# Latent attention of a two-layer trunk: second rotary product behind the first queries, latent keys' transposes one a quantum, rotary work in single steps

## The chip, the cores and the metric

One core of a Trainium2 chip runs the whole program in one launch. The metric is the device time of one execution in microseconds; the median of several runs counts. In profiles the engines are PE (TensorE matmuls; PEld its weight loads), DVE (VectorE), ACT (ScalarE), POOL (GpSimd) and SP (SyncE, which issues the DMAs).

## The reference, cut to what matters

Two decoder layers at 256 tokens, width 2048, float32. Layer 0 has block-sparse attention and a gated MLP, layer 1 has multi-head latent attention and the same kind of MLP. The change lies in the latent attention alone:

```python
cq = rms_norm(h @ wq_a, g_qa)                                # 2048 -> 512
q = (cq @ wq_b).reshape(B, S, H, NOPE + RD)                  # 16 heads of 128 + 64
q_nope = rms_norm(q[..., :NOPE], g_qn)
q_rope = rope(rms_norm(q[..., NOPE:], g_qr), pos, RD)        # RD = 64
kv_a = h @ wkv_a                                             # 2048 -> 512 + 64
ckv = rms_norm(kv_a[..., :MLA_KV_RANK], g_kva)
k_rope = rope(rms_norm(kv_a[..., MLA_KV_RANK:], g_kr)[:, :, None, :], pos, RD)[:, :, 0]
kv = (ckv @ wkv_b).reshape(B, S, H, NOPE + VD)
k_nope = rms_norm(kv[..., :NOPE], g_kn)
v = kv[..., NOPE:]
# per head: s = (q_nope k_nope + q_rope k_rope) * scale, causal; softmax; s @ v; then @ wo
```

## The kernel before, in words

**Products.** Every weight matrix is streamed from HBM in units of 1 MB (four pieces of 128 x 512; wkv_a in pieces of 128 x 288). The list `units` gives the order. For each piece ScalarE rounds a high part (`whi`, L104) and VectorE subtracts it to get a low part (`wlo`, L105); TensorE multiplies high by high, low by high and high by low. A product with one piece of weights is a quantum: six matmuls in the form of `tok_major` (L235; tokens on the partitions, weights moving), or twelve in that of `feat_major` (L261 to L263).

**Order.** The list `quanta` holds the products in order; `at(q, f)` hangs a piece of other work behind quantum q. At the end one loop writes the program out: for each quantum it first splits the weight piece that is three quanta ahead, then issues the quantum's matmuls, then all work hung at q, in the order in which it was hung. Each engine works through its instructions in this order, so a VectorE instruction that waits holds up the low parts behind it. Parts have five buffers.

**Latent attention.** Its stages in order: wq_a (feature-major, 16 quanta, gives `cqT`); the first rotary product `rotary_queries(0)` (4 quanta: 8 heads of 64); wkv_a (two halves of 16 quanta, 288 columns each, gives `ckv`); then four groups of four heads, each with queries (`mla_wqn`, from `cqT`), keys (`mla_wkn`) and values (`mla_wv`, both from `ckvT`), four quanta each. The first group takes queries first, the others keys first. The second rotary product stands ahead of the second group.

**Work around the change.** Of each product of heads, `Heads.evac` copies the sums out of PSUM on ScalarE, `squares` sums squares per head on VectorE (L379), `rstd` forms the inverse root (GpSimd's power, L392), `scaled` multiplies it in (L397, VectorE; `scaled_only`, L413, on ScalarE for the rotary queries), `rotate` applies the rotary tables on VectorE (L435 to L440), `turned` transposes on TensorE (L449) and `turned_out` copies out on ScalarE (L457, L460). For the latent keys `kva_evac`, `kva_stats`, `kva_scale` (L858, L859), `kva_rotate` (L872 to L876), `kva_turn` (transposes L881, then high and low parts L886 and L887 into `ckvT`) and `kr_turn` (transposes L894, zeroing L898, copies L899 into two tiles, `kr`) do the same. `Head.plan` hangs scores, softmax and values of a head over eight quanta.

With Q for the last quantum of wkv_a, the statistics are hung at Q, the scaling at Q+3, the turns 0 and 1 at Q+3, 2 and 3 at Q+4, the key's rotation at Q+7 and its turn, with the zeroing, at Q+9.

Of the kernel before, what the change touches and what calls it, by code (L numbers as in the profile page):

```python
# [17 lines left out]
P = 128  # L18
# [97 lines left out]
def trunk(ctx: ExitStack, tc: tile.TileContext, a, out):  # L116
# [99 lines left out]
    def at(q, f, *args):  # L216
        side.setdefault(q, []).append((f, args))
# [135 lines left out]
    class Heads:  # L353
# [19 lines left out]
                else:  # L373
                    nc.scalar.activation(dst, src, AF.Copy, scale=self.scale()[:, t : t + 1])

        def squares(self, t):
            for i in range(self.n):
                junk = att_pool.tile([P, P], F32, name="junk", bufs=2)
                nc.vector.tensor_tensor_reduce(  # L379
                    out=junk[:, : self.dh], in0=self.x[:, t, i], in1=self.x[:, t, i], scale=1.0,  # L380
                    scalar=0.0, op0=ALU.mult, op1=ALU.add, accum_out=self.ss[:, t, i : i + 1],
                )
# [9 lines left out]
            nc.gpsimd.tensor_tensor(self.r, ms, mhalf[:, : NT * n], op=ALU.pow)  # L392

        def scaled(self, t):
            if self.gain_column is not None:
                r = self.r[:, t * self.n : (t + 1) * self.n]
                nc.vector.tensor_tensor(  # L397
                    self.x[:, t], self.x[:, t], r[:, :, None].to_broadcast([P, self.n, self.dh]),
                    op=ALU.mult,
                )  # L400
                return
            g = gains[:, self.gain : self.gain + self.dh]
            for i in range(self.n):
                c = t * self.n + i
                nc.vector.scalar_tensor_tensor(
                    self.x[:, t, i], self.x[:, t, i], self.r[:, c : c + 1], g,
                    op0=ALU.mult, op1=ALU.mult,
                )

        def scaled_only(self, t, heads):  # L410
            for i in heads:
                c = t * self.n + i
                nc.scalar.activation(  # L413
                    self.x[:, t, i], self.x[:, t, i], AF.Copy, scale=self.r[:, c : c + 1]
                )

        def rotate(self, t, stages=(0, 1)):
            if not self.rot:
                return
            n, rot = self.n, self.rot  # L420
            hf = rot // 2
            tb, C, Sn = self.tabs
            ct = tb[:, C + t * rot : C + (t + 1) * rot]
            st = tb[:, Sn + t * rot : Sn + (t + 1) * rot]
            x = self.x[:, t]
            def over(s):
                return s[:, None, :].to_broadcast([P, n, s.shape[1]])

            def part(name):
                r = att_pool.tile([P, 16 * 32], F32, name=name, bufs=2)  # L430
                return r[:, : n * rot].rearrange("p (n r) -> p n r", n=n)

            if 0 in stages:
                t1, t2 = self.rot_parts = part("ro1"), part("ro2")
                nc.vector.tensor_tensor(t1, x[:, :, :rot], over(ct), op=ALU.mult)  # L435
                nc.vector.tensor_tensor(t2[:, :, :hf], x[:, :, hf:rot], over(st[:, :hf]), op=ALU.mult)
            if 1 in stages:
                t1, t2 = self.rot_parts
                nc.vector.tensor_tensor(t2[:, :, hf:], x[:, :, :hf], over(st[:, hf:]), op=ALU.mult)
                nc.vector.tensor_tensor(x[:, :, :rot], t1, t2, op=ALU.add)  # L440

        def turned(self, dst, pair, i0):
# [179 lines left out]
    def plan_heads(q, hs, key, step, out=None, late=0):  # L622

        at(q, hs.evac)
        for t in range(NT):
            at(q + step * (1 + t), hs.squares, t)
        at(q + step * 3, hs.rstd)
# [208 lines left out]
                AF.Copy, scale=n3.rstd[:, t : t + 1],  # L836
            )

    def kva_stats():
        ss = small.tile([P, NT, 2], F32, name="kvss")  # L840
        for t in range(NT):
            for k, (lo, hi) in enumerate(((0, 512), (512, 576))):
                junk = att_pool.tile([P, 512], F32, name="kvjunk", tag="ro1", bufs=2)
                nc.vector.tensor_tensor_reduce(
                    out=junk[:, : hi - lo], in0=env["ckv"][:, t, lo:hi], in1=env["ckv"][:, t, lo:hi],
                    scale=1.0 / (hi - lo), scalar=0.0, op0=ALU.mult, op1=ALU.add,
                    accum_out=ss[:, t, k : k + 1],
                )
        ms = small.tile([P, NT * 2], F32, name="kvms")
        nc.vector.tensor_scalar(ms, ss.rearrange("p t k -> p (t k)"), EPS, None, op0=ALU.add)  # L850
        env["kvr"] = small.tile([P, NT * 2], F32, name="kvr")
        nc.gpsimd.tensor_tensor(env["kvr"], ms, mhalf[:, : NT * 2], op=ALU.pow)

    def kva_scale():
        r = env["kvr"]
        for t in range(NT):
            c = env["ckv"][:, t]
            nc.vector.tensor_scalar(c[:, :512], c[:, :512], r[:, 2 * t : 2 * t + 1], None, op0=ALU.mult)  # L858
            nc.vector.scalar_tensor_tensor(  # L859
                c[:, 512:], c[:, 512:], r[:, 2 * t + 1 : 2 * t + 2], gains[:, G_KR : G_KR + 64],  # L860
                op0=ALU.mult, op1=ALU.mult,
            )

    def kva_rotate():
        env["krr"] = att_pool.tile([P, NT, 2, 64], F32, name="krr", bufs=1)
        for t in range(NT):
            x = env["ckv"][:, t, 512:]
            ct = tab[:, T_LC + t * 64 : T_LC + (t + 1) * 64]
            st = tab[:, T_LS + t * 64 : T_LS + (t + 1) * 64]
            t1 = att_pool.tile([P, 64], F32, name="kro1", bufs=2)  # L870
            t2 = att_pool.tile([P, 64], F32, name="kro2", bufs=2)
            nc.vector.tensor_tensor(t1, x, ct, op=ALU.mult)  # L872
            nc.vector.tensor_tensor(t2[:, :32], x[:, 32:], st[:, :32], op=ALU.mult)
            nc.vector.tensor_tensor(t2[:, 32:], x[:, :32], st[:, 32:], op=ALU.mult)
            for i in range(2):
                nc.vector.tensor_tensor(env["krr"][:, t, i], t1, t2, op=ALU.add)  # L876

    def kva_turn(r):
        tp = ps_tp.tile([P, 512], F32, name="tp")
# [11 lines left out]
    def kr_turn():  # L891
        tp = ps_tp.tile([P, 512], F32, name="tp")
        for t in range(NT):
            nc.tensor.transpose(  # L894
                tp[:, t * P : (t + 1) * P], env["krr"][:, t].rearrange("p i d -> p (i d)"), ident
            )
        for i in range(2):
            nc.gpsimd.memset(env["kr"][i], 0.0)  # L898
            nc.vector.tensor_copy(env["kr"][i][i * 64 : (i + 1) * 64, :], tp[i * 64 : (i + 1) * 64, :S])  # L899


# [58 lines left out]
    def rotary_queries(u, step):  # L960
        state = {}
        for kt in range(4):
            q = add(tok_major, state, lambda: env["cqT"], kt, 3)
        hs = Heads(state, 8, 64, None, 64, None, lambda: cq["scale"])

        def rotate(t, stage):
            hs.tabs = (env["gtab"].rearrange("p a r -> p (a r)"), 0, NT * 64)
# [1 line left out]

        at(q, hs.evac)  # L970
        for t in range(NT):
            at(q + step * (1 + t), hs.squares, t)
        at(q + step * 3, hs.rstd)
        for t in range(NT):
            for half in range(2):
                at(q + step * (6 + 2 * t + half), hs.scaled_only, t, range(4 * half, 4 * half + 4))
            at(q + step * (8 + 2 * t), rotate, t, 0)
            at(q + step * (9 + 2 * t), rotate, t, 1)
        for i0 in (0, 2):
            pair = {}  # L980
            at(q + step * 14 + i0 // 2, lambda p=pair, i0=i0: hs.turned(None, p, i0))
            at(q + step * 14 + i0 // 2, lambda p=pair, i0=i0: hs.turned_out(
                env["qrT"][:, 4 * u : 4 * u + 4], p, i0))
# [184 lines left out]
```

## Time and profile before

| | us |
|---|---|
| median of 3 runs (lowest to highest) | 2096.03 (2095.92 to 2097.42) |
| the profiled execution: time | 2096.73 |
| its span, first to last instruction | 2094.9 |
| PE busy | 2086.9 (100%) |
| PEld busy | 2014.8 (96%) |
| DVE busy | 1403.5 (67%) |
| ACT busy | 1137.7 (54%) |
| POOL busy | 45.6 (2%) |

A matmul's record lasts from its start to the modelled end of its pipeline, and the next one starts before that end, so records overlap; how fast TensorE goes on is read from start to start. In a timeline, a row ends with the idle time ahead of it and what ended that, in brackets, where there was any. In a group of instructions the columns are count, busy time, mean ns of one, idle time of the engine ahead of them and its releaser.

### The profile page before, as it was taken

How to read it: one execution, taken by the hardware profiler on the slowest of the kernel's cores; microseconds unless marked ns; L12 is line 12 of the kernel's file. 1: busy time of each engine (PE TensorE's matmuls, PEld its weight loads, DVE VectorE, ACT ScalarE, POOL GpSimd, SP SyncE). 2: the span in 40 equal slices, each digit the busy share in tenths (PEclk: the TensorE clock that was granted, in tenths of full speed). 3: DMA queues.
4: the chain of work that ended last, by engine and by line, in shares of the span. 5: the costliest groups of instructions: out<-in, count | busy, mean ns of one | idle time of the engine just before them, and what ended most of it. 6: DMA issues, size and time to landing. Idle time of an engine off the chain costs nothing.

```text
span 2094.9 us, 42206 instructions
## 1 busy us (share of the span) xinstructions
PE 2086.9 (100%) x16716; PEld 2014.8 (96%) x16716; DVE 1403.5 (67%) x3072; ACT 1137.7 (54%) x2238; POOL 45.6 (2%) x37
## 2 busy tenths in 40 slices
PE   9999999999999999999999999999999999999999
PEld 7888889999999999999999889999999999999999
DVE  6777776777666676655556786776766667755554
ACT  6555555555555555555555675655555555544443
POOL 0000000000000000000000110000000000000000
PEclk9999999999999999999999999999999999999999
DMA  7454445555555555555554533555555555555553
GB/s 273 161 181 176 167 163 200 181 202 185 198 195 189 201 191 192 202 195 190 201 189 152 185 129 117 185 183 200 193 191 201 189 195 199 186 204 209 195 206 131
DMA packets 59382, 391.83 MB, mean 187 GB/s; under 512 B 6960, under 2 KB 10032, under 8 KB 13232
## 3 DMA queue, kind: packets, MB, share of 16 engines
q1 hardware_dynamic: 59040, 388.87, 52.3%
q8 instruction: 131, 2.15, 0.4%
q14 instruction: 67, 0.55, 0.1%
q10 hardware_dynamic: 144, 0.26, 0.1%
HBM read 387.01 MB, written 2.10 MB: 186 GB/s over the span
## 4 chain that ended last, share of the span: by engine, by line
PE 98%; DVE 1%; DMA 0%; SPq 0%; issue 0%; ACT 0%; POOL 0%; POOLq 0%; ACTq 0%
PE acc L261 26%; PE acc L263 26%; PE acc L262 26%; PE acc L235 17%; PE tp L449 1%; PE sc L489 1%; PE tp L521 1%; PE sc L486 0%; PE sc L546 0%; DVE wlo L105 0%; DMA xT<-in_xT 0%; PE sc L465 0%; PE sc L466 0%; PE sc L464 0%; PE sc L544 0%; PE sc L547 0%
## 5 line engine op out<-in xcount | busy, mean ns | idle before, releaser
L105 DVE TENSOR_TENSOR wlo<-raw,whi 128x512 fp32r<-128x512 f32 (+1 forms) x1480 | 1000.8, 684 | 394.2 <-ACT whi L104 391.3
L104 ACT CAST whi<-raw 128x512 fp32r<-128x512 f32 (+1 forms) x1479 | 871.9, 614 | 459.6 <-PE acc L262 213.7
L261 PE MATMUL acc<-h,whi 128*128 128x256 f32 x2880 | 796.1, 276 | 0.0
L263 PE MATMUL acc<-h,wlo 128*128 128x256 f32 x2880 | 795.7, 276 | 0.0
L262 PE MATMUL acc<-h,whi 128*128 128x256 f32 x2880 | 795.6, 276 | 0.0
L262 PEld LDWEIGHTS acc<-h,whi 128*128 128x128 f32 x2880 | 540.8, 188 | 0.0
L261 PEld LDWEIGHTS acc<-h,whi 128*128 128x128 f32 x2880 | 540.8, 188 | 0.0
L263 PEld LDWEIGHTS acc<-h,wlo 128*128 128x128 f32 x2880 | 540.8, 188 | 0.0
L262 PE MATMUL acc<-a,whi 128*128 128x256 f32 x1408 | 389.0, 276 | 0.0
L261 PE MATMUL acc<-a,whi 128*128 128x256 f32 x1408 | 389.0, 276 | 0.0
L263 PE MATMUL acc<-a,wlo 128*128 128x256 f32 x1408 | 389.0, 276 | 0.0
L235 PE MATMUL acc<-whi,h 128*128 128x512 f32 (+1 forms) x896 | 274.3, 380 | 0.6 <-ACT whi L104 0.6
L261 PEld LDWEIGHTS acc<-a,whi 128*128 128x128 f32 x1408 | 264.4, 188 | 0.0
L263 PEld LDWEIGHTS acc<-a,wlo 128*128 128x128 f32 x1408 | 264.4, 188 | 0.0
L262 PEld LDWEIGHTS acc<-a,whi 128*128 128x128 f32 x1408 | 264.4, 188 | 0.0
L235 PEld LDWEIGHTS acc<-whi,h 128*128 128x128 f32 x896 | 164.7, 188 | 30.9 <-ACT whi L104 1.4
L235 PE MATMUL acc<-wlo,h 128*128 128x512 f32 (+1 forms) x448 | 169.4, 378 | 0.5 <-DVE wlo L105 0.4
L261 PE MATMUL acc<-oT,whi 128*128 128x256 f32 x512 | 144.9, 283 | 0.0
L263 PE MATMUL acc<-oT,wlo 128*128 128x256 f32 x512 | 141.9, 277 | 0.0
L262 PE MATMUL acc<-oT,whi 128*128 128x256 f32 x512 | 141.7, 277 | 0.0
L740 DVE TENSOR_TENSOR g<-acc,rstd_b 128x256 f32<-128x256 f32 x88 | 37.5, 426 | 125.6 <-PE acc L263 122.7
L747 ACT ACTIVATE c<-g,par 128x256 f32<-128x256 f32 x88 | 53.1, 603 | 108.0 <-DVE g L740 108.0
(160 smaller groups left out, 1602.2 us busy)
## 6 DMA issues: line engine op xcount, KB each, us to landing
raw<-in_ffn_gu SPq DMA_DIRECT2D x176, 1024.0 KB, 4.8
raw<-in_ffn_down SPq DMA_DIRECT2D x88, 1024.0 KB, 4.8
raw<-in_moba_wk SPq DMA_DIRECT2D x16, 1024.0 KB, 4.8
raw<-in_moba_wv SPq DMA_DIRECT2D x16, 1024.0 KB, 4.8
raw<-in_moba_wo SPq DMA_DIRECT2D x16, 1024.0 KB, 4.8
raw<-in_mla_wo SPq DMA_DIRECT2D x16, 1024.0 KB, 4.8
raw<-in_moba_wq SPq DMA_DIRECT2D x13, 1024.0 KB, 4.9
raw<-in_mla_wkv_a SPq DMA_DIRECT2D x8, 576.0 KB, 3.7
```

The source lines that it names most:

```text
L104: self.nc.scalar.copy(hi[:, :n], w)
L105: self.nc.vector.tensor_tensor(lo[:, :n], w, hi[:, :n].bitcast(F32), op=ALU.subtract)
L235: mm(state["acc"][t][:, :n], src[:, kt, c : c + P], (t_lo if part == 1 else t_hi)[:, :n], start=kt == 0 and part == 0, stop=kt == k_last a ...
L261: mm(o, w_hi, src[:, kt, :S], start=first and k == 0, stop=False, skip_group_check=True)
L262: mm(o, w_hi, src[:, kt, S:], start=False, stop=False, skip_group_check=True)
L263: mm(o, w_lo, src[:, kt, :S], start=False, stop=kt == k_last, skip_group_check=True)
L449: nc.tensor.transpose(tp[:, (i * NT + t) * P : (i * NT + t + 1) * P], flat[:, t, c : c + P], ident)
L489: mm(o, qr[:, q0 : q0 + P], kr[:, :n], start=False, stop=True)
L521: nc.tensor.transpose(tp[:, c * P : (c + 1) * P], self.s[:, c * P : (c + 1) * P], ident)
L740: nc.vector.tensor_tensor(self.g[:, 2:], self.gate["acc"][:, :S], self.norm.rstd_b, op=ALU.mult)
L747: nc.scalar.activation(self.c, self.g[:, 2:], AF.Identity, bias=par[:, cb : cb + 1], scale=self.cw(2))
```

## The change

The order of weights in the first group becomes queries, second rotary product, keys, values:

```diff
     for g in range(4):
-        if g == 1:
-            units += grouped("mla_wqr", 1, 1)
-        for name in ("mla_wkn", "mla_wqn", "mla_wv") if g else ("mla_wqn", "mla_wkn", "mla_wv"):
-            units += grouped(name, 1, g)
+        names = ("mla_wkn", "mla_wqn", "mla_wv") if g else ("mla_wqn", "mla_wqr", "mla_wkn", "mla_wv")
+        for name in names:
+            units += grouped(name, 1, 1 if name == "mla_wqr" else g)
...
     for g in range(4):
-        if g == 1:
-            rotary_queries(1, 2)
-        for kind in "kqv" if g else "qkv":
+        for kind in "kqv" if g else "qrkv":
+            if kind == "r":
+                rotary_queries(1, (6, 8, 10, 12, 13, 16, 18, *range(20, 36, 2), 36, 37))
+                continue
...
-                plan_heads(q, hs, ("qT" if kind == "q" else "kT", g), 1)
+                plan_heads(q, hs, ("qT" if kind == "q" else "kT", g), 1, wide=(g, kind) == (0, "q"))
```

The first queries' squares are taken two heads at a time, and their steps lie further apart:

```diff
         at(q, hs.evac)
+        if wide:
+            for t in range(NT):
+                for i in (0, 2):
+                    at(q + 1 + 2 * t + i // 2, hs.squares, t, range(i, i + 2))
+                at(q + 8 + t, hs.scaled, t)
+            at(q + 5, hs.rstd)
+            for i0 in (0, 2):
+                pair = {}
+                q1 = q + 11 + i0 // 2
+                at(q1, lambda p=pair, i0=i0: hs.turned(env[key], p, i0))
+                at(q1, lambda p=pair, i0=i0: hs.turned_out(env[key], p, i0))
+            return
```

The rotary queries are scaled by one VectorE operation for each half of the tokens, in place of eight on ScalarE; squares come four heads at a time, the rotation's four operations each at a quantum of its own, and every step has its place in a list:

```diff
         def scaled(self, t):
-            if self.gain_column is not None:
+            if self.gain_column is not None or self.gain is None:
...
-        def scaled_only(self, t, heads):
...
-        def rotate(self, t, stages=(0, 1)):
+        def rotate(self, t, stages=range(4)):
...
-    at(q_start + 20, gained_tables)
+    at(q_start + 10, gained_tables)
...
         for t in range(NT):
-            at(q + step * (1 + t), hs.squares, t)
-        at(q + step * 3, hs.rstd)
-        for t in range(NT):
-            for half in range(2):
-                at(q + step * (6 + 2 * t + half), hs.scaled_only, t, range(4 * half, 4 * half + 4))
-            at(q + step * (8 + 2 * t), rotate, t, 0)
-            at(q + step * (9 + 2 * t), rotate, t, 1)
+            for i in (0, 4):
+                at(next(steps), hs.squares, t, range(i, i + 4))
+        at(next(steps), hs.rstd)
+        for t in range(NT):
+            at(next(steps), hs.scaled, t)
+        for t in range(NT):
+            for stage in range(4):
+                at(next(steps), rotate, t, stage)
...
-    rotary_queries(0, 2)
+    rotary_queries(0, (2, 3, 5, 6, 8, 12, 14, 17, 18, 20, 21, 23, 24, 26, 27, 30, 31))
```

`kva_stats` becomes `kva_squares` for each half of wkv_a and `kva_rstd`; the key's gain and rotation become `kr_rotate(t)` for each half of the tokens; the zeroing becomes `kr_clear`. Their places:

```diff
         at(q, kva_evac, state, half)
+        at(q + (0 if half else 1), kva_squares, half)
...
     at(q, open_room)
-    at(q, kva_stats)
+    at(q, kva_rstd)
+    at(q + 1, kr_clear)
     at(q + 3, kva_scale)
-    at(q + 7, kva_rotate)
     for r in range(4):
-        at(q + 3 + r // 2, kva_turn, r)
-    at(q + 9, kr_turn)
+        at(q + 5 + r, kva_turn, r)
+    for t in range(NT):
+        at(q + 9 + t, kr_rotate, t)
+    at(q + 13, kr_turn)
```

More of the change, by code (lines that the diff above doesn't have):

```diff
@@ L374, in evac, with squares @@
                     nc.scalar.activation(dst, src, AF.Copy, scale=self.scale()[:, t : t + 1])
-        def squares(self, t):
-            for i in range(self.n):
+        def squares(self, t, heads=None):
+            for i in heads or range(self.n):
                 junk = att_pool.tile([P, P], F32, name="junk", bufs=2)
@@ L620, in evac_values, with plan_heads @@
                 nc.scalar.activation(dst, src, AF.Copy, scale=scale()[:, t : t + 1])
-    def plan_heads(q, hs, key, step, out=None, late=0):
+    def plan_heads(q, hs, key, step, out=None, late=0, wide=False):
         at(q, hs.evac)
+        if wide:
[10 more added lines that the diff above has]
+            return
         for t in range(NT):
@@ L837, in kva_evac, with kva_squares @@
             )
-    def kva_stats():
-        ss = small.tile([P, NT, 2], F32, name="kvss")
+    def kva_squares(half):
+        if half == 0:
+            env["kvss"] = small.tile([P, NT, 3], F32, name="kvss")
+        cols = ((0, 0, KVN),) if half == 0 else ((1, KVN, 512), (2, 512, 576))
         for t in range(NT):
-            for k, (lo, hi) in enumerate(((0, 512), (512, 576))):
+            for k, lo, hi in cols:
                 junk = att_pool.tile([P, 512], F32, name="kvjunk", tag="ro1", bufs=2)
@@ L851, in kva_stats, with kva_rstd @@
+                    accum_out=env["kvss"][:, t, k : k + 1],
+                )
+    def kva_rstd():
+        ss = env["kvss"]
+        ms = small.tile([P, NT, 2], F32, name="kvms")
+        nc.vector.scalar_tensor_tensor(
+            ms[:, :, 0], ss[:, :, 0], EPS, ss[:, :, 1], op0=ALU.add, op1=ALU.add
+        )
+        nc.vector.tensor_scalar(ms[:, :, 1], ss[:, :, 2], EPS, None, op0=ALU.add)
         env["kvr"] = small.tile([P, NT * 2], F32, name="kvr")
-        nc.gpsimd.tensor_tensor(env["kvr"], ms, mhalf[:, : NT * 2], op=ALU.pow)
+        nc.gpsimd.tensor_tensor(
+            env["kvr"], ms.rearrange("p t k -> p (t k)"), mhalf[:, : NT * 2], op=ALU.pow
+        )
@@ L854, in kva_scale @@
     def kva_scale():
-        r = env["kvr"]
         for t in range(NT):
             c = env["ckv"][:, t]
[L858 to L861, printed above, removed]
-            )
-    def kva_rotate():
-        env["krr"] = att_pool.tile([P, NT, 2, 64], F32, name="krr", bufs=1)
-        for t in range(NT):
[L867 to L876, printed above, removed]
+            nc.vector.tensor_scalar(
+                c[:, :512], c[:, :512], env["kvr"][:, 2 * t : 2 * t + 1], None, op0=ALU.mult
+            )
@@ new lines, in kr_clear, with kr_rotate @@
+    def kr_clear():
+        for kr in env["kr"]:
+            nc.gpsimd.memset(kr, 0.0)
+    def kr_rotate(t):
+        if t == 0:
+            env["krr"] = att_pool.tile([P, NT, 2, 64], F32, name="krr", bufs=1)
+        x = env["ckv"][:, t, 512:]
+        nc.vector.scalar_tensor_tensor(
+            x, x, env["kvr"][:, 2 * t + 1 : 2 * t + 2], gains[:, G_KR : G_KR + 64],
+            op0=ALU.mult, op1=ALU.mult,
+        )
+        ct = tab[:, T_LC + t * 64 : T_LC + (t + 1) * 64]
+        st = tab[:, T_LS + t * 64 : T_LS + (t + 1) * 64]
+        t1 = att_pool.tile([P, 64], F32, name="kro1", bufs=2)
+        t2 = att_pool.tile([P, 64], F32, name="kro2", bufs=2)
+        nc.vector.tensor_tensor(t1, x, ct, op=ALU.mult)
+        nc.vector.tensor_tensor(t2[:, :32], x[:, 32:], st[:, :32], op=ALU.mult)
+        nc.vector.tensor_tensor(t2[:, 32:], x[:, :32], st[:, 32:], op=ALU.mult)
+        for i in range(2):
+            nc.vector.tensor_tensor(env["krr"][:, t, i], t1, t2, op=ALU.add)
@@ L956, in gained_tables, with rotary_queries @@
         nc.vector.tensor_tensor(gt[:, NT:, 32:], ts_[:, :, 32:], over(g[:, :32]), op=ALU.mult)
-    at(q_start + 20, gained_tables)
-    def rotary_queries(u, step):
+    at(q_start + 10, gained_tables)
+    def rotary_queries(u, steps):
         state = {}
@@ L964, in rotary_queries @@
         hs = Heads(state, 8, 64, None, 64, None, lambda: cq["scale"])
+        steps = iter(q + n for n in steps)
         def rotate(t, stage):
@@ L971, in rotary_queries @@
         for t in range(NT):
-            at(q + step * (1 + t), hs.squares, t)
-        at(q + step * 3, hs.rstd)
+            for i in (0, 4):
+                at(next(steps), hs.squares, t, range(i, i + 4))
+        at(next(steps), hs.rstd)
         for t in range(NT):
-            for half in range(2):
-                at(q + step * (6 + 2 * t + half), hs.scaled_only, t, range(4 * half, 4 * half + 4))
-            at(q + step * (8 + 2 * t), rotate, t, 0)
-            at(q + step * (9 + 2 * t), rotate, t, 1)
+            at(next(steps), hs.scaled, t)
+        for t in range(NT):
+            for stage in range(4):
+                at(next(steps), rotate, t, stage)
         for i0 in (0, 2):
             pair = {}
-            at(q + step * 14 + i0 // 2, lambda p=pair, i0=i0: hs.turned(None, p, i0))
-            at(q + step * 14 + i0 // 2, lambda p=pair, i0=i0: hs.turned_out(
-                env["qrT"][:, 4 * u : 4 * u + 4], p, i0))
-    rotary_queries(0, 2)
+            n = next(steps)
+            at(n, lambda p=pair, i0=i0: hs.turned(None, p, i0))
+            at(n, lambda p=pair, i0=i0: hs.turned_out(env["qrT"][:, 4 * u : 4 * u + 4], p, i0))
+    rotary_queries(0, (2, 3, 5, 6, 8, 12, 14, 17, 18, 20, 21, 23, 24, 26, 27, 30, 31))
     for half in range(2):
```

20 lines of the change are left out of this document (7 added, 13 removed).

## The prediction

> **What bounds the kernel now.** The page comes first, then the busy times by stage, then TensorE's own timeline where a stage shows a gap.
>
> ```profile
> span 2094.9 us, 42206 instructions
> PE 2086.9 (100%) x16716; PEld 2014.8 (96%) x16716; DVE 1403.5 (67%) x3072; ACT 1137.7 (54%) x2238; POOL 45.6 (2%) x37
> PE 98%; DVE 1%; DMA 0%; SPq 0%; issue 0%; ACT 0%; POOL 0%; POOLq 0%; ACTq 0%
> ```
>
> TensorE bounds the kernel from end to end: it is busy 2086.9 of 2094.9 us and carries 98% of the chain that ended last. The change adds and removes no matmul. So all that it can win is time in which TensorE waits, and only in the latent attention. The windows bracket that stage: the latent keys' down-projection (wkv_a), the first latent group, and the rest up to the output projection.
>
> ```profile
> 1136.20:1163.40 27.20, 27.14 (x202) 26.37 (x201) 19.31 (x75) 19.31 (x55) 2.98 (x1) 1.00 0.59 194
> 1163.40:1190.00 26.60, 24.49 (x113) 19.01 (x112) 22.24 (x83) 15.67 (x30) 5.78 (x5) 1.00 0.46 167
> 1190.00:1266.60 76.60, 76.60 (x404) 65.07 (x404) 60.85 (x265) 54.78 (x136) 12.40 (x6) 1.00 0.37 131
> ```
>
> Columns: length, then busy time of PE, PEld, DVE, ACT, POOL, and the granted clock, which is 1.00 throughout. TensorE is idle for 2.1 us in the middle stretch and not at all in the last. VectorE is 84% busy in the middle stretch (22.24 of 26.60). Busy time hides short waits, because a matmul lasts longer than the step to the next one, so I take steps from start to start on TensorE's timeline (time, duration, what).
>
> ```profile
> 1136.18 0.29 PE L235 MATMUL acc<-whi,h 128*128 128x288 f32 x1
> ...
> 1142.72 0.29 PE L235 MATMUL acc<-wlo,h 128*128 128x288 f32 x1
> ...
> 1151.02 0.29 PE L235 MATMUL acc<-wlo,h 128*128 128x288 f32 x1
> ...
> 1159.21 0.29 PE L235 MATMUL acc<-whi,h 128*128 128x288 f32 x1
> ...
> 1159.92 0.29 PE L235 MATMUL acc<-wlo,h 128*128 128x288 f32 x1
> ...
> 1163.38 0.39 PE L235 MATMUL acc<-whi,cqT 128*128 128x512 f32 x1
> ...
> 1167.26 0.39 PE L235 MATMUL acc<-whi,cqT 128*128 128x512 f32 x1
> 1168.40 0.30 PE L881 MATMUL tp<-ident,ckv 128*128 128x128 f32 x1 [0.76 <-DVE ckv L858]
> ...
> 1169.21 0.47 PE L235 MATMUL acc<-whi,cqT 128*128 128x512 f32 x1
> ...
> 1170.21 0.39 PE L235 MATMUL acc<-wlo,cqT 128*128 128x512 f32 x1
> 1170.44 0.39 PE L235 MATMUL acc<-whi,cqT 128*128 128x512 f32 x1
> ...
> 1171.03 0.48 PE L235 MATMUL acc<-whi,ckvT 128*128 128x512 f32 x1
> ...
> 1177.72 0.39 PE L235 MATMUL acc<-whi,ckvT 128*128 128x512 f32 x1
> ...
> 1178.84 0.48 PE L235 MATMUL acc<-whi,ckvT 128*128 128x512 f32 x1
> ...
> 1183.03 0.39 PE L235 MATMUL acc<-whi,cqT 128*128 128x512 f32 x1
> 1184.23 0.50 PE L235 MATMUL acc<-wlo,cqT 128*128 128x512 f32 x1 [0.81 <-DVE wlo L105]
> 1184.56 0.62 PE L235 MATMUL acc<-whi,cqT 128*128 128x512 f32 x2
> ```
>
> An undisturbed 512-column matmul steps on after 0.23 us (1170.21 to 1170.44). The sum of what is lost:
> - Latent keys' transposes. From the last matmul ahead of them to the product behind, the undisturbed group takes 0.59 us (1170.44 to 1171.03), the first group 1.95 us (1167.26 to 1169.21). Loss **1.36 us**: VectorE scales the latent keys (L858) and TensorE turns them in the same quantum.
> - Rotary key's transposes. The step over them is 1.12 us (1177.72 to 1178.84). Two transposes instead of four would take about 0.37 us by the undisturbed group (0.23 plus half of the remaining 0.36, minus rounding). Loss **0.75 us**.
> - The step from 1183.03 to 1184.23 is 1.20 instead of 0.23, and the next 0.33 instead of 0.23. Loss **1.07 us**: the low part of a weight piece (L105) came late from VectorE.
> - wkv_a lasts 27.20 us (1136.18 to 1163.38). From 1142.72 to 1151.02 lie 21 groups of three matmuls, 0.395 us each; the stage has 16 pieces of six matmuls for each of its two halves, so 64 groups and 25.29 us. The two rotary turns inside it cost 0.45 us each (1159.21 to 1159.92 is 0.71 for two matmuls that need 0.26). Loss **1.01 us**, in waits of about 0.1 to 0.2 us.
>
> Together 4.2 us, 0.20% of the time; that is the ceiling. As it happens, 0.2% (4.2 us) is also about what a measurement of this kernel can tell from no change.
>
> **The change part by part.** I call the last quantum of wkv_a Q; a quantum of the following products is six 512-column matmuls, 1.37 us. Each quantum's weight piece is split three quanta ahead by ScalarE (high) and VectorE (low), so VectorE may fall behind by some 4 us before TensorE waits; what stands ahead of a low part in VectorE's queue is what counts.
>
> ```profile
> 1162.35 1.90 DVE L105 TENSOR_TENSOR wlo<-raw,whi 128x512 fp32r<-128x512 f32 x3 [0.96 <-ACT whi L104]
> ...
> 1165.96 1.89 DVE L105 TENSOR_TENSOR wlo<-raw,whi 128x512 fp32r<-128x512 f32 x3
> 1167.78 0.48 DVE L858 TENSOR_SCALAR ckv<-ckv,kvr 128x512 f32<-128x512 f32 x1
> ...
> 1177.14 0.23 DVE L872 TENSOR_TENSOR kro<-ckv,tab 128x64 f32<-128x64 f32 x1
> ...
> 1178.34 0.36 DVE L876 TENSOR_TENSOR krr<-kro,kro 128x64 f32<-128x64 f32 x2
> ...
> 1181.15 0.86 DVE L899 COPY room<-tp 64x256 f32<-64x256 f32 x2 [1.18 <-POOL room L898]
> ...
> 1188.43 0.69 DVE L397 TENSOR_TENSOR qk<-qk,hr 128x512 f32<-128x512 f32 x1 [0.92 <-POOL hr L392]
> ```
>
> ```profile
> 1142.76 2.98 POOL L392 TENSOR_TENSOR hr<-hms,mhalf 128x16 f32<-128x16 f32 x1 [7.66 <-DVE hms L387]
> 1166.13 1.39 POOL L852 TENSOR_TENSOR kvr<-kvms,mhalf 128x4 f32<-128x4 f32 x1 [20.40 <-DVE kvms L850]
> 1178.92 1.94 POOL L392 TENSOR_TENSOR hr<-hms,mhalf 128x8 f32<-128x8 f32 x1 [11.40 <-DVE hms L387]
> 1180.82 0.55 POOL L898 MEMSET room<- 128x256 f32 x2
> ```
>
> The groups of VectorE from 1163 us on and of ScalarE from 1133 us on, both to 1200 us (count, then busy us and mean ns of one):
>
> ```profile
> L379 DVE CUSTOM_DVE_ANT_0 junk<-qk 128x128 f32<-128x128 f32 x16 | 3.7, 290 | 0.0
> L379 DVE CUSTOM_DVE_ANT_0 junk<-qr 128x64 f32<-128x64 f32 x16 | 2.5, 220 | 0.0
> ...
> L104 ACT CAST whi<-raw 128x512 fp32r<-128x512 f32 x24 | 13.8, 624 | 1.6 <-PE acc L235 1.6
> L374 ACT ACTIVATE qr<-acc,cscale 128x512 f32<-128x512 f32 x4 | 2.7, 688 | 2.4 <-PE acc L235 2.4
> L886 ACT ACTIVATE ckvT<-tp,par 128x256 fp32r<-128x256 f32 x4 | 1.7, 470 | 4.0 <-PE tp L881 4.0
> ```
>
> 1. *Latent keys' turns, one a quantum, from Q+5 instead of two at Q+3.* The scaling stays at Q+3; it started at 1167.78 and lasts four short steps, so it ends near 1169.0, and Q+5 ends at 1163.38 + 5 x 1.37 = 1170.2. Half of the squares moves ahead of the stage's end, which brings it earlier still. The wait goes: 1.36 us. Four groups of two transposes instead of two of four cost nothing, since the step scales with the transposes. The latent keys are read first at Q+9 now (the second rotary product fills Q+5 to Q+8), and their fourth part, turned at Q+8, only at Q+12.
> 2. *Rotary key.* It is rotated half at Q+9, half at Q+10, and turned at Q+13, three quanta (4 us) behind work of some 0.9 us. The wait goes: 0.75 us.
> 3. *The zeroing moves to Q+1.* Now VectorE waits 1.18 us at 1181.15 for a memset that stands behind a 1.94 us power on GpSimd, and the late low part at 1184.23 is behind that in VectorE's queue. At Q+1 the memsets follow the 1.39 us power and nobody needs them before Q+13. The 1.07 us go if nothing else takes that place, which is the next point.
> 4. *VectorE's load from Q+9 to Q+18.* It still has the key's rotation (0.9 us twice), its copies (0.86), the queries' scaling (0.69 twice), squares of queries, keys and now of the second rotary queries. I follow the low part of each quantum against the start of its product, from the end of Q+8. TensorE starts Q+12 at 0.22 (the fourth turn) + 3 x 1.37 = 4.3 us. VectorE is done with Q+12's low part at 0.22 + 0.47 (ScalarE's copy of that turn) + 1.37 (evacuation of the rotary product, 2 x 0.688) + 0.62 (high part) + 0.69 = 3.4: lead 1.0. With full durations (low part 0.69, a square 3.7/16 or 2.5/16, so 0.92 for four heads of 128 and 0.63 for four of 64; half the key's rotation 0.78 from 1177.14 to 1178.70, plus its scaling, 0.93) the next are:
>    - Q+13 and Q+14: 1.6 us of VectorE each against 1.37, and the key's turn of 0.22 on TensorE: lead 0.6 both times; Q+15: the low part alone, 1.3.
>    - Q+16: 1.4 against 1.37 and a queries' turn of 0.45: 1.7.
>    - Q+17: copies 0.86, scaling 0.69, squares 0.92, low part 0.69, together 3.2, against 1.82: 0.4.
>    - Q+18: squares 0.92 and 0.63, low part 0.69, together 2.2, against 1.37: -0.5.
>
>    Operations overlap a little when back to back (three low parts in 1.89, not 2.07); with such steps the smallest lead is +0.5. The cost lies between 0 and 1.2 us (the 0.5, some 0.3 at the turn of Q+15, whose queries are scaled in the same stretch, and as much again behind); I take **0.5**.
> 5. *Rotary scaling from ScalarE to VectorE, squares and rotation in single steps.* ScalarE loses 32 short operations; VectorE gains four of 0.69 us, two of them in wkv_a. There the low parts and the rotary work now alternate (each rotation step stands alone between low parts instead of in pairs), and the gained tables move 10 quanta ahead to where VectorE has room. A lead of three 0.79 us quanta covers a single 0.69 us step. Of the 1.01 us I take back **0.7**, between 0 and 1.0.
> 6. *Second rotary product 12 quanta earlier.* The weights' order in memory queue and program change together, so the DMA stream on SP's queue keeps its pace: one 1 MB unit for four quanta either way. The first group's heads come four quanta later, still ahead of the second group's. In the last window TensorE never waits although VectorE is 79% busy there, so neither gain nor loss.
>
> Sum: 1.36 + 0.75 + 1.07 + 0.7 - 0.5 = 3.4 us. The profiled execution took 2096.73 us (span 2094.9 and 1.8 around it), so it would become 2093.3; the median of the three runs is 0.7 lower, 2096.03, and becomes **2092.6**.
>
> A rule that speaks against this: the Trainium skill, SBUF — State Buffer, section "SBUF: two separate sides", says that VectorE and GpSimd share a port pair as an exclusive lock, held for a whole instruction, so that a VectorE operation with two SBUF inputs stands still beside a GpSimd one that reads SBUF. This trace disagrees: the three low parts at 1165.96 took 1.89 us beside the 1.39 us power, and three at 1162.35 took 1.90 with GpSimd idle. By that rule the two 1.94 us powers, at Q+9 and Q+15, would exceed a lead of 1.0 us by 0.9 each, and the 3.4 us would be 1.5.
>
> **The rivals.**
> - *Everything goes, and no new wait.* All 4.2 us are won and the regular steps keep their pace: 2091.8, with noise of the measurement a little either side. For it: with back-to-back steps no lead of point 4 is negative. Against: it takes every 0.1 us wait of wkv_a too.
> - *The waits change places.* VectorE's lead is used up between Q+13 and Q+18 (point 4's upper end, 1.2 us) and wkv_a gains nothing: 1.36 + 0.75 + 1.07 - 1.2 = 2.0, so 2094.0; if VectorE in addition stands still for the two 1.94 us powers less a lead of 1.0 each, 2094.0 + 1.9, near 2096, no gain. Against standing still: the two equal rows of low parts (1.90 and 1.89 us). The lock of the Trainium skill's SBUF page is what would make it stand still.
> - *Slower: VectorE sits on a power.* Rotary scaling now stands in VectorE's queue, with the low parts behind it, where ScalarE used to wait. If VectorE has no lead when it gets there, the power's time lands on TensorE: 2.98 for each rotary product, 1.94 for first queries and keys, 1.39 for the latent keys, 11.2 us in all; less the 4.2 won, 7.0 slower, 2103.0. It decides from the point where a power is longer than the quanta between it and its scaling plus the lead: in wkv_a 2.98 against four quanta of 0.79 us, 3.16, which is close; behind it, 1.94 against two or three of 1.37. Against is the chain of waits (start, length, what), which at the time of VectorE's wait of 0.92 us for a power (1188.43) shows 18 products without a gap:
>
> ```profile
> 1188.13 4.13 PE acc L235 x18
> ```
>
> - *It does not do what it says*: if the order of units and of quanta differed, weights would be wrong; both lists put the rotary unit behind the first queries, so no.
>
> **How the numbers follow.** Forecast (won 2.5 to 4.1 us): 0.58. All won or a trace more, past 0.2%: 0.24. Waits change places: 0.12, 0.02 of it with VectorE standing still. Slower: 0.06, of which 0.05 by over 0.2%. So faster by over 0.2% 0.24, within 0.2% 0.71, slower 0.05. The range takes the ceiling and 0.4 of scatter below (2091.4) and the first form of changed places and its scatter above (2095.4).
>
> **What would show it.** Right: between the wkv_a products and the output projection TensorE shows no releaser; the step over the first latent turn is near 0.4 us; VectorE's copy of the rotary key no longer waits for GpSimd; the middle stretch, with the same matmuls, is about 2.9 us shorter and wkv_a near 26.5. Wrong: a gap ahead of a low part between Q+13 and Q+18, a wait of VectorE for a power followed by one of TensorE, or gaps in a stage that the change does not touch.

## The result, and the profile after

| | before | after |
|---|---|---|
| median of 14 runs (lowest to highest), us | 2096.34 (2095.71 to 2097.56) | 2092.56 (2091.39 to 2093.98) |
| the profiled execution: time, us | 2096.73 | 2092.50 |
| its span, us | 2094.9 | 2090.7 |

The ratio is 0.998, with a 95% interval of 0.9973 to 0.9987: 3.8 us less by the medians, 4.2 us by the two profiled executions. The interval is 2.7 to 5.7 us and takes in both. It is a gain clear of the scatter and just inside 0.2%. The forecast was 2092.6.

The page of the changed kernel, busy time first: VectorE has as much to do as before (1403.5 then), ScalarE 7 us less (1137.7), and TensorE is what it was, the bound.

```profile
PE 2084.0 (100%) x16716; PEld 2014.7 (96%) x16716; DVE 1405.2 (67%) x3081; ACT 1130.9 (54%) x2206; POOL 46.0 (2%) x37
```

The middle window of the changed kernel (length, busy time of PE, PEld, DVE, ACT, POOL, clock, DMA). It has the same bounds as before, but the changed kernel reaches each product earlier, so the work in it is not quite the same. TensorE's idle time in it, 2.1 us before, is gone, although VectorE is busier (23.74 instead of 22.24).

```profile
1163.40:1190.00 26.60, 26.60 (x127) 21.87 (x126) 23.74 (x101) 18.39 (x36) 5.79 (x5) 1.00 0.46 164
```

TensorE's timeline of the changed kernel: first product of wkv_a, the group of three matmuls with the one wait left in it (from 1151.87 to the next group at 1152.55), first product of the queries, the matmuls around a turn of the latent keys and around the turn of the rotary key, the first matmul that reads the low part of Q+18, and the first product of the output projection.

```profile
1136.20 0.29 PE L234 MATMUL acc<-whi,h 128*128 128x288 f32 x1
...
1151.87 0.42 PE L234 MATMUL acc<-whi,h 128*128 128x288 f32 x2
...
1152.55 0.42 PE L234 MATMUL acc<-whi,h 128*128 128x288 f32 x2
...
1162.64 0.39 PE L234 MATMUL acc<-whi,cqT 128*128 128x512 f32 x1
...
1169.24 0.39 PE L234 MATMUL acc<-whi,cqT 128*128 128x512 f32 x1
...
1169.61 0.48 PE L234 MATMUL acc<-whi,cqT 128*128 128x512 f32 x1
...
1181.10 0.39 PE L234 MATMUL acc<-whi,ckvT 128*128 128x512 f32 x1
...
1181.47 0.48 PE L234 MATMUL acc<-whi,ckvT 128*128 128x512 f32 x1
...
1188.19 0.39 PE L234 MATMUL acc<-wlo,ckvT 128*128 128x512 f32 x1
...
1262.84 0.36 PE L260 MATMUL acc<-oT,whi 128*128 128x256 f32 x1
```

The last of these in the kernel before:

```profile
1267.04 0.36 PE L261 MATMUL acc<-oT,whi 128*128 128x256 f32 x1
```

So wkv_a takes 26.44 us instead of 27.20, and the way from there to the output projection 100.20 instead of 103.66 (1267.04 less 1163.38). From the first product of wkv_a to the first of the output projection it is **126.64 instead of 130.86 us, 4.22 less**; behind it both kernels take the same 827.9 us to the end of the span. I call this distance the stage. The steps over the turns are 0.37 us (1169.24 to 1169.61, 1181.10 to 1181.47), with no releaser.

VectorE and GpSimd of the changed kernel:

```profile
1146.07 0.69 DVE L396 TENSOR_TENSOR qr<-qr,hr 128x512 f32<-128x512 f32 x1 [0.84 <-POOL hr L391]
...
1165.00 1.90 DVE L105 TENSOR_TENSOR wlo<-raw,whi 128x512 fp32r<-128x512 f32 x3
...
1182.69 0.85 DVE L921 COPY room<-tp 64x256 f32<-64x256 f32 x2
...
1187.05 0.69 DVE L105 TENSOR_TENSOR wlo<-raw,whi 128x512 fp32r<-128x512 f32 x1
```

```profile
1165.17 1.39 POOL L868 TENSOR_TENSOR kvr<-kvms,mhalf 128x4 f32<-128x4 f32 x1 [19.14 <-DVE kvms L866]
```

The copies of the rotary key wait for nobody now. The low part of Q+18 is ready at 1187.74 (1187.05 and 0.69) and first read at 1188.19: 0.45 us to spare, the thinnest place behind wkv_a. In wkv_a the low part at 1152.32 comes with nothing to spare; that is the one wait left.

### The profile page after: what moved, and what is told of

It is laid out like the page before. It is cut to its first block, busy times and chain, and to the rows that moved or that the text cites. A ratio compares the mean times of both kernels' runs of the same rounds, so it can differ in the third digit from the quotient of the medians.

```text
span 2090.7 us, 42183 instructions
## 1 busy us (share of the span) xinstructions
PE 2084.0 (100%) x16716; PEld 2014.7 (96%) x16716; DVE 1405.2 (67%) x3081; ACT 1130.9 (54%) x2206; POOL 46.0 (2%) x37
## 4 chain that ended last, share of the span: by engine, by line
PE 99%; DMA 0%; SPq 0%; DVE 0%; ACT 0%; issue 0%
PE acc L260 26%; PE acc L262 26%; PE acc L261 26%; PE acc L234 17%; PE tp L444 1%; PE tp L516 1%; PE sc L484 1%; PE sc L481 1%; PE sc L541 0%; DMA xT<-in_xT 0%; PE sc L460 0%; PE sc L461 0%; PE sc L459 0%; PE sc L539 0%; PE sc L542 0%; PE sc L476 0%
```

## The experiments

Whole times of one kernel scatter by 1.5 to 3 us (the kernel before took 2095.71 to 2098.75), and nearly all of that lies ahead of wkv_a, whose first product came between 1135.59 and 1137.74 us in the executions below. The stage hardly scatters: two executions of one kernel (the last below) gave 126.34 and 126.35 us, 26.15 of it for wkv_a both times. Most kernels below were run once. So I read the stage or its wkv_a part from each trace. Rows are TensorE's first product of wkv_a, of the queries, or of the output projection, unless said otherwise.

**Turns back beside the scaling.**

```diff
-        at(q + 5 + r, kva_turn, r)
+        at(q + 3 + r // 2, kva_turn, r)
```

> The changed kernel with the latent keys' turns back at Q+3 (two) and Q+4 (two). Measure: from the first wkv_a product to the first product of the output projection, 130.86 us before and 126.64 after. Theory (the wait is the short distance from scaling to turn): the scaling ran from 1166.81 to 1167.73 in the changed kernel and Q+3 ends near 1166.73, so about 1.0 us comes back, in the step over the first turn alone: 127.6. Rival (it was the late squares that made TensorE wait, and taking half of them early is enough): at most 0.2 us, 126.8.

```profile
1137.21 0.29 PE L234 MATMUL acc<-whi,h 128*128 128x288 f32 x1
...
1167.53 0.39 PE L234 MATMUL acc<-whi,cqT 128*128 128x512 f32 x1
1168.49 0.85 PE L904 MATMUL tp<-ident,ckv 128*128 128x128 f32 x4 [0.58 <-DVE ckv L875]
1169.10 0.47 PE L234 MATMUL acc<-whi,cqT 128*128 128x512 f32 x1
...
1264.79 0.36 PE L260 MATMUL acc<-oT,whi 128*128 128x256 f32 x1
```

Stage 127.58, 0.94 lost, and the step over the turn is 1.57 instead of 0.59 us. The theory holds, the rival falls: even with half of the squares early the scaling is too late for a turn in its own quantum.

**Zeroing back in the rotary key's turn.**

```diff
-    at(q + 1, kr_clear)
...
         for i in range(2):
+            nc.gpsimd.memset(env["kr"][i], 0.0)
             nc.vector.tensor_copy(env["kr"][i][i * 64 : (i + 1) * 64, :], tp[i * 64 : (i + 1) * 64, :S])
```

> The changed kernel with the zeroing back in the rotary key's turn, now at Q+13. Same measure. Theory (the zeroing cost something because it stood behind a power on GpSimd): the queries' power ended at 1180.80 and the turn is at 1181.33, so GpSimd is free, the two memsets take 0.56 us, VectorE gets to its copies only at 1182.69: no loss, 126.6. Rival (late zeroing costs VectorE a wait wherever the turn stands): VectorE waits some 0.5 us ahead of the copies and the thin leads behind them turn into 0.3 to 0.6 us, 127.0 to 127.2.

```profile
1137.74 0.29 PE L234 MATMUL acc<-whi,h 128*128 128x288 f32 x1
...
1264.35 0.36 PE L260 MATMUL acc<-oT,whi 128*128 128x256 f32 x1
```

```profile
1180.39 1.94 POOL L391 TENSOR_TENSOR hr<-hms,mhalf 128x8 f32<-128x8 f32 x1 [12.29 <-DVE hms L386]
...
1182.28 0.56 POOL L921 MEMSET room<- 128x256 f32 x2
...
1184.22 0.85 DVE L922 COPY room<-tp 64x256 f32<-64x256 f32 x2
```

Stage 126.61: nothing lost. The memsets still come right behind the queries' power, which ends at 1182.33. They are over at 1182.84, and VectorE gets to the copies, which now stand four quanta later, 1.4 us after that.

**The zeroing alone moved, in the kernel before.** (`kr_clear` at Q+1, nothing else.)

> The kernel before with the zeroing alone moved to Q+1. Same measure, 130.86 before. Theory (VectorE's wait of 1.18 us for the memset behind the power made the low part late): that wait and the 1.07 us behind it go, with the small steps after it 1.1 to 1.3 us: 129.6 to 129.8. Rival (VectorE, 84% busy there, is overloaded and the low part is late in any case): at most 0.3 us, 130.6.

```profile
1135.92 0.29 PE L235 MATMUL acc<-whi,h 128*128 128x288 f32 x1
...
1265.68 0.36 PE L261 MATMUL acc<-oT,whi 128*128 128x256 f32 x1
```

Stage 129.76, 1.10 less. With the run before this tells the mechanism: it is not the zeroing that costs, but the short way from the queries' power, and the zeroing behind it, to the copies. In the kernel before it pays to take it away; in the changed one the turn at Q+13 leaves room for both, and it could have stayed.

**The latent keys' squares in two halves, in the kernel before.** (`kva_squares` and `kva_rstd` of the changed kernel; all else as before.)

> The kernel before with the latent keys' squares taken in two halves, the first half behind the first half of wkv_a; turns stay at Q+3. Same measure, 130.86 before. Theory (the wait lasts from the end of Q+3 to the end of the scaling, so what starts the scaling earlier shortens it by as much): the scaling starts 0.7 to 0.9 us earlier and the loss of 1.36 us shrinks to some 0.5 to 0.7: 130.0 to 130.2. Rival (the wait is set by something else in VectorE's queue, the low parts ahead of the scaling): no change, 130.8.

```profile
1135.73 0.29 PE L235 MATMUL acc<-whi,h 128*128 128x288 f32 x1
...
1163.81 0.39 PE L235 MATMUL acc<-whi,cqT 128*128 128x512 f32 x1
...
1266.84 0.36 PE L261 MATMUL acc<-oT,whi 128*128 128x256 f32 x1
```

Stage 131.11, 0.25 longer than before: a miss, though half of the theory holds. Behind wkv_a 0.63 us are won (103.03 instead of 103.66), near what the theory says, but wkv_a itself takes 28.08 instead of 27.20: the early squares come in the midst of the rotation in pairs. So alone they cost more than they win. In the changed kernel the same squares stand between single steps and cost 0.29 us (the last run below). That the single steps make the room is what this comparison suggests; no run has the one without the other.

**VectorE's lead spent on purpose.** One, then two useless multiplications at Q+14.

```diff
+    def extra():
+        for _ in range(1):        # 2 in the second run
+            t = att_pool.tile([P, 512], F32, name="extra", tag="ro1", bufs=2)
+            nc.vector.tensor_tensor(t, env["ckv"][:, 0, :512], env["ckv"][:, 1, :512], op=ALU.mult)
+
+    at(q + 14, extra)
```

> The changed kernel with one useless VectorE multiplication of 512 columns (about 0.65 us) hung at Q+14, ahead of the low part of Q+18. Measure: first wkv_a product to first product of the output projection, 126.63 after. Theory (VectorE's lead is what the change spends, and it is down to about 0.2 us at Q+18, 0.43 against the first matmul that reads the low part): 0.2 to 0.35 us lost, 126.85 to 127.0. Rival (VectorE has room enough, its lead decides nothing): 126.6.

> As the run with one useless multiplication, with two of them (about 1.25 us). Theory: every further microsecond of VectorE lands on TensorE, 0.7 to 0.95 us lost, 127.3 to 127.6. Rival: 126.6 to 126.8.

TensorE in the first run and in the second:

```profile
1135.59 0.29 PE L234 MATMUL acc<-whi,h 128*128 128x288 f32 x1
...
1262.57 0.36 PE L260 MATMUL acc<-oT,whi 128*128 128x256 f32 x1
```

```profile
1136.45 0.29 PE L234 MATMUL acc<-whi,h 128*128 128x288 f32 x1
...
1189.26 0.49 PE L234 MATMUL acc<-wlo,ckvT 128*128 128x512 f32 x1 [0.65 <-DVE wlo L105]
...
1264.05 0.36 PE L260 MATMUL acc<-oT,whi 128*128 128x256 f32 x1
```

Stages 126.98 and 127.60: 0.34 and 0.96 lost, both as the theory says. The first 0.65 us cost half, the second (1.29 together) nearly all: VectorE's lead at Q+18 was the room left, some 0.3 to 0.45 us, and what goes beyond it lands on TensorE.

**The order of products back.** Keys follow the queries again; turns at Q+4 to Q+7; the second rotary queries' steps in the places where they end as before.

```diff
-        names = ("mla_wkn", "mla_wqn", "mla_wv") if g else ("mla_wqn", "mla_wqr", "mla_wkn", "mla_wv")
+        names = ("mla_wkn", "mla_wqn", "mla_wv") if g else ("mla_wqn", "mla_wkn", "mla_wv", "mla_wqr")
...
-        at(q + 5 + r, kva_turn, r)
+        at(q + 4 + r, kva_turn, r)
...
-        for kind in "kqv" if g else "qrkv":
+        for kind in "kqv" if g else "qkvr":
             if kind == "r":
-                rotary_queries(1, (6, 8, 10, 12, 13, 16, 18, *range(20, 36, 2), 36, 37))
+                rotary_queries(1, (2, 2, 4, 4, 6, 12, 14, 16, 16, 18, 18, 20, 20, 22, 22, 28, 29))
```

> The changed kernel with the second rotary product back behind the first group, so that keys follow the queries at Q+5; the latent keys' turns are hung one a quantum at Q+4 to Q+7, the latest at which each is there for its product. The second rotary queries' steps are set closer, to end where they ended before. Measure as above, 126.63 after. Theory (the rotary product is there to put distance between turn and use): each turn is followed at once by the product that reads it, which waits for ScalarE's copy, about 0.5 us four times, 128.4 to 129.2. Rival (one turn a quantum is enough by itself): 126.6 to 126.9.

```profile
1137.02 0.29 PE L234 MATMUL acc<-whi,h 128*128 128x288 f32 x1
...
1168.69 0.39 PE L234 MATMUL acc<-whi,cqT 128*128 128x512 f32 x1
...
1169.86 0.50 PE L234 MATMUL acc<-whi,ckvT 128*128 128x512 f32 x1 [0.56 <-ACT ckvT L909]
...
1189.46 0.55 PE L444 MATMUL tp<-ident,qk 128*128 128x128 f32 x3 [0.43 <-DVE qk L396]
...
1267.97 0.36 PE L260 MATMUL acc<-oT,whi 128*128 128x256 f32 x1
```

Stage 130.95, 4.3 lost: the direction is the theory's, the size is above its range (128.4 to 129.2). The step over each turn is 1.17 instead of 0.37 us (1168.69 to 1169.86), so a turn read at once costs 0.8 us and not 0.5, four times, and a turn of the queries waits for their scaling as well. So turns one a quantum need the rotary product in between: without it this form of the change loses behind wkv_a more than it won there, and only the 0.77 us in wkv_a stay. What the order of products is worth with the turns in another place is not known. In the kernel before, with turns at Q+3 and Q+4, each was a quantum or more ahead of the keys that read it, and the changed kernel loses only 0.94 with its turns there (the first run above). That place with the keys behind the queries, and all else changed, was not run.

**Rotary scaling back on ScalarE**, eight operations in a step, then four in a step at the old quanta. The first run's edit (`scaled_only` is that of the kernel before, over all eight heads; the second run gives it four heads and the first product's old places):

```diff
-            at(next(steps), hs.scaled, t)
+            at(next(steps), hs.scaled_only, t)      # ScalarE: Copy with scale, head by head
```

> The changed kernel with the rotary queries scaled on ScalarE again, eight short operations at each of the two steps; all other steps as in the changed kernel. Measure: the wkv_a stage, first to last product, 27.20 us before and 26.44 after. Theory (the stage was held up by the rotary work's engine: ScalarE's short operations of about 0.27 us each, 2.1 us a step, delay the high parts): 26.7 to 27.0. Rival (what counted is that VectorE's rotary steps stand one by one and the tables earlier): 26.4.

> The changed kernel with the rotary queries scaled on ScalarE in steps of four heads, at the quanta where the kernel before had them; the rest as in the changed kernel. Measure: wkv_a stage, 27.20 us before, 26.44 after. With eight at a time it was 28.95. Theory (what lengthens the stage is a block longer than the lead, not the engine: four operations take 1.06 us, under the lead of three 0.79 us quanta): 26.4 to 26.6. Rival (short operations on ScalarE delay the high parts in any step): 27.0 or more.

The first run:

```profile
1136.38 0.29 PE L234 MATMUL acc<-whi,h 128*128 128x288 f32 x1
...
1165.34 0.39 PE L234 MATMUL acc<-whi,cqT 128*128 128x512 f32 x1
```

The second run, TensorE and then ScalarE:

```profile
1136.56 0.29 PE L234 MATMUL acc<-whi,h 128*128 128x288 f32 x1
...
1154.22 0.40 PE L234 MATMUL acc<-wlo,h 128*128 128x288 f32 x1 [0.80 <-DVE wlo L105]
...
1164.55 0.39 PE L234 MATMUL acc<-whi,cqT 128*128 128x512 f32 x1
```

```profile
1146.42 1.07 ACT L412 ACTIVATE qr<-qr,hr 128x64 f32<-128x64 f32 x4 [1.33 <-POOL hr L391]
```

ScalarE at the same step of the kernel before:

```profile
1145.77 1.07 ACT L413 ACTIVATE qr<-qr,hr 128x64 f32<-128x64 f32 x4 [0.57 <-POOL hr L392]
```

wkv_a takes 28.96 and 27.99 us, 2.5 and 1.5 more than with VectorE. The first goes the way of its theory but lies 2 us above its range. The second is a miss of the theory, and its rival (27.0 or more) is right. Both are also above the kernel before (27.20), which scaled on ScalarE in the same places as the second run. What differs there: ScalarE waits 1.33 us for the power in these runs and 0.57 in the kernel before, because the power starts some 0.3 us later in wkv_a (6.85 us from its first product instead of 6.58) and ScalarE comes to it some 0.5 us earlier; and the early squares meet the late rotation. The second run's trace shows where the time goes: some 0.8 us at 1151.43 to 1152.60, where first the high part and then the low part is late, and 1.07 at 1153.13 to 1154.46, where the low part stands behind a rotation step and the two early squares. No run has one without the other.

**The power two quanta later** (the 8 in the first list of steps made 10).

> The changed kernel with the first rotary product's power two quanta (1.58 us) later, the scaling where it was. VectorE waited 0.84 us for that power in the changed kernel, without a wait of TensorE; now it waits about 2.4 us. Measure: wkv_a stage, 26.44 us after. Theory (the forecast's slower rival: a wait of VectorE costs what exceeds its lead; the low part behind the scaling was about 1.0 us early): 0.4 to 0.7 us lost, 26.85 to 27.15. Rival (waits for a power never reach TensorE here): 26.4 to 26.5.

```profile
1135.91 0.29 PE L234 MATMUL acc<-whi,h 128*128 128x288 f32 x1
...
1162.35 0.39 PE L234 MATMUL acc<-whi,cqT 128*128 128x512 f32 x1
```

```profile
1146.51 0.69 DVE L396 TENSOR_TENSOR qr<-qr,hr 128x512 f32<-128x512 f32 x1 [1.58 <-POOL hr L391]
```

wkv_a 26.44: nothing lost. But VectorE's wait grew by 0.74 us only and not by 1.58: it runs ahead of TensorE, and the two quanta were for it two low parts, 0.83 us; 0.74 is under the lead of 1.0. So the point from which a power's wait reaches TensorE was not reached: inconclusive on the threshold, and it shows that the forecast's slower rival had room to spare here.

**The last wait of wkv_a.** The first half's squares move from the quantum behind the half to the third.

```diff
-        at(q + (0 if half else 1), kva_squares, half)
+        at(q + (0 if half else 3), kva_squares, half)
```

> The changed kernel with the first half of the latent keys' squares two quanta later, at a quantum without a rotary step. Measure: the wkv_a stage, 26.44 us after. Theory (the one wait left in that stage, 0.29 us at 1152.00, is two squares of 288 columns right behind a rotary step of 512): it goes, 26.15. Rival (the low parts would be late there from the rotary steps alone): 26.4.

```profile
1136.06 0.29 PE L234 MATMUL acc<-whi,h 128*128 128x288 f32 x1
...
1162.21 0.39 PE L234 MATMUL acc<-whi,cqT 128*128 128x512 f32 x1
```

wkv_a 26.15, as the theory says: the 0.29 us at 1152.00 are gone. Timed against the kernel before:

> The changed kernel with the first half of the latent keys' squares two quanta later, timed. By the stage it is 0.29 us shorter than the changed kernel, far below what whole times can tell apart: 4.1 us under the kernel before, ratio 0.998. If the interval took in 1.000, the gain of the change itself would be in doubt.

2092.18 us (median of 11) against 2096.70 (of 15), ratio 0.9978, interval 0.9969 to 0.9987. It beats the kernel before; the 0.29 us over the changed kernel show in the traces, while the whole times (2092.18 and 2092.56) cannot tell them apart.

## Why the prediction was right

The mechanism was right: TensorE bounds, and the change can only take its waits away. The signs that the prediction named came: no releaser on TensorE in the stage, steps of 0.37 us over the turns, copies without a wait for GpSimd, wkv_a at 26.44 (near 26.5), no gap between Q+13 and Q+18. One was off in size: behind wkv_a 3.46 us were won, not "about 2.9", and by the prediction's own terms that figure should have been 2.7 (1.36, 0.75 and 1.07 less 0.5). Point by point, against the stage's 4.22 us:

- *Turns (1.36) and rotary key (0.75)*: both steps are at their undisturbed length now. Putting only the turns back loses 0.94 of the 1.36 again. The other 0.42 is about what the scaling ends earlier: 5.09 us behind the first product of the queries (1167.73 less 1162.64) instead of 5.47 (1168.85 less 1163.38). It starts 0.23 earlier, and the key's gain no longer stands between its two halves. Whether the changed kernel needs the early squares no run shows: its scaling is over 1.7 us ahead of the first turn (1169.47).
- *Zeroing and the late low part (1.07)*: 1.10 by itself in the kernel before. The reason given, the wait behind the power, was right; that the move was needed was not, since the later place of the copies had already made room.
- *VectorE's lead (-0.5)*: the mis-sized term; it cost nothing. The leads forecast with full durations were right to some 0.2 us up to Q+16; at Q+17 and Q+18, with their many short squares, they were too low by what back-to-back operations overlap. For Q+18, -0.5 was forecast at the quantum's start, and the low part was ready 0.45 us ahead of its first reader, one matmul (0.23) behind that start, so +0.2. The end with overlapping steps, +0.5, was the nearer one. That VectorE's lead is what counts there was right: 0.65 us more cost 0.34, 1.3 cost 0.96.
- *wkv_a (0.7 of 1.01)*: 0.76. The size was right; what lies under it was only half seen. An undisturbed group of three matmuls takes 0.395 us. The groups of the kernel before that take longer lie in two places, one behind the gained tables and squares of eight heads in a row (0.55 us at 1140.00, 0.72 at 1141.74, so 0.48 too long), the other beside the rotation in pairs (0.61 at 1153.16, 0.49 at 1154.95, 0.62 at 1156.63, so 0.54 too long). The longest:

```profile
1141.74 0.42 PE L235 MATMUL acc<-whi,h 128*128 128x288 f32 x2
...
1142.46 0.42 PE L235 MATMUL acc<-whi,h 128*128 128x288 f32 x2
```

Both places are free of them in the changed kernel, and the early squares add 0.29. So by the traces it was the tables' earlier place, the squares in fours and the single rotation steps that won; the first place is free in both runs with the scaling on ScalarE too. None of the three was run alone. At ScalarE's scaling the kernel before shows no such group: moving it to VectorE took no wait away, but kept off 1.5 us or more that the scaling costs ScalarE among the change's other steps (28.96 and 27.99).
- *Missing from the sum*: the second low part behind the late one in the kernel before. The two steps from 1185.84 to 1186.62 take 0.78 us, and 0.54 in the next such place (1187.89 to 1188.43), so some 0.24 is lost. Behind wkv_a the stage won 3.46 where 1.36, 0.75 and 1.07 make 3.18.

So the forecast's 3.4, with 0.5 for the lead, 0.28 that was missing and 0.06 in wkv_a, make the 4.22 of the trace: nearly all was won, the case that had 0.24. By the medians it is 3.8 us, inside the forecast's own case (2.5 to 4.1), with an interval that takes in both. That the forecast time met the median to 0.1 us is partly luck: the three runs it started from had a median 0.3 under that of fourteen, and the gain was taken 0.4 too small.

The rule of the Trainium skill that spoke against the change (SBUF — State Buffer, "SBUF: two separate sides", the lock on the port that VectorE and GpSimd share) does not show here either: three low parts at 1165.00 beside the power at 1165.17 took 1.90 us, as the three at 1162.35 of the kernel before did with GpSimd idle.

## What to carry to other kernels

Where one engine is busy to the end, add up what its steps from start to start lose against undisturbed ones: that sum is an estimate of what a change of order can win. Here it was 4.2 us, and 4.22 were won, though not part for part: some 0.25 of wkv_a's loss stayed, and 0.28 came that the sum had missed. Put distance, in quanta of the bounding engine, between a result and its reader, and check in the helper's queue what stands ahead of the next thing that engine needs; cost that queue by steps back to back, not by durations. A move that helps in one order (the zeroing) may be idle in another, and one that hurts alone (the early squares) may cost less among others (0.29 us instead of 0.88 in wkv_a).

## What the runs showed of the hardware

The same work repeats closely from execution to execution. wkv_a took 26.43 to 26.45 us in the seven executions above whose kernels differ there in nothing, or only in the place of the power. The stage took 126.34 and 126.35 in the two of one kernel, and the rest behind it 827.8 to 827.9 us but for one kernel (827.5). Whole times scatter by 1.5 to 3 us: the scatter of this kernel lies in what comes before. Two transposes that the next product reads at once take 1.17 us from the matmul ahead of them to that product, in place of 0.37; the 0.8 lost is more than the 0.47 of ScalarE's copy alone.
